# Splitting the FFN head's weights during the output projection, and adding layer 0's last squares on GpSimd

## The chip, the cores and the metric

The kernel runs on one core of a Trainium2 chip. The metric is device time in microseconds (us), from runs of the whole kernel; smaller is better. Five engines matter: TensorE (PE, with its weight load PEld), VectorE (DVE), ScalarE (ACT), GpSimd (POOL) and SyncE (SP), whose queue issues the loads. Each works through its own list of instructions in order, and semaphores tie the lists together.

## The reference, cut to what matters

Two sequences, a prompt of 256 tokens and a sample of 512, go through the same two-layer encoder in float32. Layer 0 mixes with an mLSTM, layer 1 with sliding-window attention; both end in an output projection and are followed by a convolutional feed-forward network (FFN).

```python
for l in range(DEPTH):                                   # 2 layers, d = 1024
    sh1, sc1, g1, sh2, sc2, g2 = split(silu(c) @ adaln_w[l] + adaln_b[l], 6)
    h = rmsnorm(x, norm_g[l, 0]) * (1 + sc1) + sh1
    y = mlstm_mixer(h, ...) if l == 0 else swa_mixer(h, ...)   # both end in "@ w_out"
    x = x + g1 * y
    h = rmsnorm(x, norm_g[l, 1]) * (1 + sc2) + sh2
    x = x + g2 * conv_ffn(h, w_up[l], conv_w[l], conv_b[l], w_down[l])
return rmsnorm(x, final_g)

def conv_ffn(h, w_up, conv_w, conv_b, w_down):           # 1024 -> 2 * 2816 -> 1024
    u = depthwise_conv3(h @ w_up, conv_w) + conv_b
    return (silu(u[..., :D_FF]) * u[..., D_FF:]) @ w_down

def rmsnorm(x, g):
    return x * rsqrt(mean(x * x, axis=-1) + 1e-6) * g
```

## The kernel before

The 768 tokens lie along the free dimension; channels lie on the 128 partitions, eight blocks of them (KC = 8). A float32 product is made of three matmuls: every operand is split into a high part, rounded by a cast on ACT, and a low part, the subtraction of the high part on DVE (`fp_copy_split`, L223 to L234: the cast is L232, the subtraction L233). Weights come in units of 128 x 1024 by `load` (L241) into five `raw` buffers, and `split` writes their parts into three pairs `whi`, `wlo`.

A planner orders most of the program: it lays the instructions of each engine by its own estimates of their times, so that an operation that is given to another engine also changes where its neighbours stand. In `head` the lists of PE, ACT and DVE are kept in the order in which the code is written (`manual_schedule`), while POOL and SP stay with the planner.

The places that matter here are these.

- `out_proj` (L558): the output projection of a layer, 16 tiles of 24 matmuls, eight for tokens 0 to 383, then eight for tokens 384 to 767. Each tile is followed by its residual on DVE (L557) and the square of the new x on ACT (L104); six of eight squares are summed by five adds (L108), and a mean on PE (`pa<-inv,nt`), the reciprocal root on POOL (L127, `nr`) and a broadcast on PE (`pa<-kct,nr`) make the norm's factor. The generator hands control back once, ahead of its last tile.
- `head` (L1184): the start of the FFN's first pair of up-projections. It multiplies in quarters, by a Strassen-like scheme: T1, T2, T3, T4, B22 are combinations of quarters of the activations (`zh`, `zl` hold their parts; `yh`, `yl` those of the first half), and five sums and differences of weight quarters (`sums`, L1220 to L1225) take the place of further products. `wa`, `wb`, `wc` are split weights of the pair's two units. Four products of whole weights with the first half, the outsets, start before the second half's norm is known: with wa[0], wa[1], ahead[0] and ahead[1]. While they run, the second half's norm advances step by step on DVE and ACT: T1 (four steps), four scalings, T2, T4, B22, T3 (L1054 to L1100, the low parts at L1072).
- In layer 0 the output projection reads its input from other buffers, so that `zh` and `zl` are free until the quarters are written; in layer 1 it reads `zh` and `zl` themselves.
- `ffn`, `down` (from L1362): the down-projection of the last part. Per range of 256 tokens, eight tiles of six matmuls, residual, square, add, and then the norm of the next layer (layer 0) or of the output (layer 1). The norm of layer 1 writes `zh`, `zl` with L517 (scaling on DVE), L519 (ACT) and L520 (the low part on DVE).
- After layer 0's FFN comes the attention's input projection; around its first tiles DVE and ACT also work on its keys and bias (L825 to L864).

## Time and profile before

| what | value |
|---|---|
| median of 3 runs | 1913.54 us (1912.68 to 1914.77) |
| profiled execution | 1916.43 us |
| its span, first to last instruction | 1914.6 us (1.8 us lie around it) |
| mean granted TensorE clock | 0.987 |
| PE busy | 1832.8 us (96%) |
| DVE, ACT, POOL busy | 1402.9, 909.9, 473.9 us |

The stages that the change touches lie, by the trace's timeline, at 452 to 527 us (layer 0's output projection), 523 to 564 (its FFN's head), 1030 to 1100 (the end of layer 0's FFN and the start of the attention's projection), 1302 to 1367 (layer 1's output projection) and 1363 to 1405 (its head). A row of a timeline has the start, the duration, the engine, the line, the operation with its output and inputs by the program's names, the shape, the count, and in brackets the idle time of the engine ahead of it with what ended it. A row of windows has a stretch of time, its length, the busy time of PE, PEld, DVE, ACT and POOL with the number of instructions, the granted clock, the busy share of the DMA engines and their GB/s.

### The profile page before, as it was taken

Reading aid. Unit: us, or ns where it says so; the run is one execution under the profiler, and the core shown is the slowest. Engines: PE = TensorE matmul, PEld = TensorE weight load, DVE = VectorE, ACT = ScalarE, POOL = GpSimd, SP = SyncE. Lnnn points to the kernel's source line nnn. Section 1 sums busy time; section 2 is a strip of 40 time slices with the busy share of each in tenths; the row PEclk is TensorE's granted clock in tenths of the full one; section 3 lists DMA queues with packets and bytes.
Section 4 is the critical chain, followed back from the end, with each engine's and each line's share of the span. In section 5 each row is a group of like instructions: output and inputs, shape, how many; then the busy total and the mean of one; then the engine's idle time right before and its main releaser. Section 6 shows DMA issues by size and latency. Waiting matters only on the chain.

```text
span 1914.6 us, 29030 instructions
## 1 busy us (share of the span) xinstructions
PE 1832.8 (96%) x11270; PEld 1668.4 (87%) x11270; DVE 1402.9 (73%) x2311; ACT 909.9 (48%) x1832; POOL 473.9 (25%) x372
## 2 busy tenths in 40 slices
PE   6999999999999999999999899999989999999997
PEld 4978887889988999999999798778979999999996
DVE  4765577685699777777777855775997777777777
ACT  3444333433564444444444555674565444444443
POOL 2101001021023333333331011331133333333322
PEclk9999999999999999999999899999999999999998
DMA  8343466455222212122223221122222222222112
GB/s 327 108 149 126 148 202 201 160 170 182 67 68 71 69 58 67 66 68 69 71 69 101 80 68 60 40 88 67 89 77 67 67 69 69 72 67 67 66 34 67
DMA packets 63957, 183.43 MB, mean 96 GB/s; under 512 B 6135, under 2 KB 23799, under 8 KB 63820
## 3 DMA queue, kind: packets, MB, share of 16 engines
q1 hardware_dynamic: 63820, 181.58, 28.9%
q8 instruction: 88, 1.44, 0.3%
q14 instruction: 49, 0.40, 0.1%
HBM read 175.13 MB, written 6.43 MB: 95 GB/s over the span
## 4 chain that ended last, share of the span: by engine, by line
PE 78%; DVE 10%; issue 4%; DMA 3%; ACT 3%; POOL 1%; SPq 0%; POOLq 0%; ACTq 0%; DVEq 0%
PE pa L226 25%; PE ps L226 23%; PE ps L1114 9%; PE ps L1115 9%; PE ps L1116 9%; PE pa L953 2%; DVE wlo L233 2%; DVE slab L557 1%; DMA raw<-in_adaln_w_dram 1%; DVE slab L1332 1%; ACT whi L232 1%; DVE zl L1072 1%; DMA slab<-in_x_dram 1%; DMA raw<-in_w_dram 1%; DMA slab<-in_adaln_w_dram 1%
## 5 line engine op out<-in xcount | busy, mean ns | idle before, releaser
L232 ACT CAST whi<-raw 128x1024 fp32r<-128x1024 f32 x237 | 248.4, 1049 | 419.4 <-PE pa L226 201.5
L233 DVE TENSOR_TENSOR wlo<-raw,whi 128x1024 fp32r<-128x1024 f32 x237 | 325.1, 1373 | 136.8 <-ACT whi L232 135.6
L226 PE MATMUL pa<-slab,whi 128*128 128x256 f32 (+1 forms) x1472 | 346.5, 332 | 5.7 <-DVE slab L557 5.5
L226 PEld LDWEIGHTS pa<-slab,whi 128*128 128x128 f32 x1472 | 252.2, 189 | 32.7 <-DVE slab L557 7.5
L557 DVE SCALAR_TENSOR_TENSOR slab<-pa,mod,slab 128x256 f32<-128x256 f32 (+1 forms) x368 | 207.3, 590 | 65.7 <-PE pa L226 65.4
L226 PE MATMUL ps<-zh,whi 128*128 128x256 f32 (+2 forms) x688 | 229.6, 337 | 5.3 <-ACT whi L232 4.3
L226 PE MATMUL pa<-slab,wlo 128*128 128x256 f32 (+1 forms) x736 | 234.5, 331 | 0.0
L226 PE MATMUL ps<-zh,wlo 128*128 128x256 f32 (+2 forms) x688 | 229.5, 337 | 3.8 <-DVE wlo L233 3.8
L226 PE MATMUL ps<-zl,whi 128*128 128x256 f32 (+2 forms) x688 | 230.0, 336 | 0.0
L1114 PE MATMUL ps<-zh,whi 128*128 128x384 f32 x504 | 171.6, 341 | 16.6 <-ACT ps L1169 15.5
L1115 PE MATMUL ps<-zl,whi 128*128 128x384 f32 x504 | 170.9, 339 | 1.3 <-DVE zl L1072 1.0
L1116 PE MATMUL ps<-zh,wlo 128*128 128x384 f32 x504 | 169.7, 337 | 0.0
L226 PEld LDWEIGHTS pa<-slab,wlo 128*128 128x128 f32 x736 | 139.2, 189 | 13.4 <-DVE wlo L233 0.9
L226 PEld LDWEIGHTS ps<-zh,whi 128*128 128x128 f32 x688 | 132.4, 193 | 18.6 <-ACT whi L232 6.0
L226 PEld LDWEIGHTS ps<-zh,wlo 128*128 128x128 f32 x688 | 132.9, 193 | 14.9 <-DVE wlo L233 4.6
L226 PEld LDWEIGHTS ps<-zl,whi 128*128 128x128 f32 x688 | 132.8, 194 | 10.7 <-issue 1.5
L1358 POOL TENSOR_TENSOR slab<-slab 128x772 f32<-128x772 f32 x44 | 83.6, 1901 | 205.6 <-DVE slab L1332 192.9
L1145 POOL TENSOR_TENSOR raw<-raw,raw 128x512 f32<-128x512 f32 x40 | 52.7, 1317 | 294.0 <-DVE wlo L233 244.1
L1331 DVE SCALAR_TENSOR_TENSOR slab<-slab,cstt,slab 128x771 f32<-128x771 f32 x88 | 103.5, 1178 | 26.9 <-ACT slab L1329 26.9
L1332 DVE SCALAR_TENSOR_TENSOR slab<-slab,cstt,slab 128x771 f32<-128x771 f32 x88 | 120.4, 1368 | 0.8
L476 DVE SCALAR_TENSOR_TENSOR ada<-raw,silc,ada 128x1024 f32<-128x1024 f32 x84 | 111.3, 1357 | 7.4 <-DMA raw<-in_adaln_w_dram 7.0
L1114 PEld LDWEIGHTS ps<-zh,whi 128*128 128x128 f32 x504 | 95.0, 189 | 24.5 <-ACT ps L1169 20.6
(301 smaller groups left out, 4149.6 us busy)
## 6 DMA issues: line engine op xcount, KB each, us to landing
raw<-in_w_dram SPq DMA_DIRECT2D x206, 512.0 KB, 3.7
raw<-in_adaln_w_dram SPq DMA_DIRECT2D x84, 512.0 KB, 4.4
slab<-in_x_dram SPq DMA_DIRECT2D x12, 512.0 KB, 8.3
slab<-in_adaln_w_dram SPq DMA_DIRECT2D x12, 512.0 KB, 10.2
slab<-mrows SPq DMA_DIRECT2D x8, 384.0 KB, 5.2
xs<-slab SPq DMA_DIRECT2D x6, 512.0 KB, 3.4
bt<-brow SPq DMA_DIRECT2D x16, 192.0 KB, 3.1
slab<-xs SPq DMA_DIRECT2D x6, 512.0 KB, 8.0
```

The source lines that it names most:

```text
L226: self.nc.tensor.matmul(out, lhsT, rhs, start=start, stop=stop)
L232: nc.scalar.copy(hi, src)
L233: return nc.vector.tensor_tensor(lo, src, hi.bitcast(F32), ALU.subtract)
L476: stt(acc[:, s], row, w, acc[:, s], ALU.mult, ALU.add)
L557: self.nc.vector.scalar_tensor_tensor(x, o, self.mod[l][:, gc + c, q : q + 1], x, ALU.mult, ALU.add)
L1114: mm(o, wh[:, k], hi[k], start=start and k == 0, stop=False, skip_group_check=True)
L1115: mm(o, wh[:, k], lo[k], start=False, stop=False, skip_group_check=True)
L1116: mm(o, wl[:, k], hi[k], start=False, stop=k == 3, skip_group_check=True)
L1145: tt(q[0], q[2], q[0], ALU.subtract)
L1331: stt(y[:, 1:], u[:, :-1], w(0), y[:, 1:], ALU.mult, ALU.add)
L1332: stt(y[:, :-1], u[:, 1:], w(2), y[:, :-1], ALU.mult, ALU.add)
L1358: nc.gpsimd.tensor_tensor(y, y, yrow[:, j], ALU.mult)
```

## The change

There are three edits.

1. `out_proj` hands control back once more, after its first eight tiles, and `ffn` first calls the new `prepare`, then goes on with the projection. `prepare` splits weights of the head: wa[1] (there wa2), and in layer 0 also ahead[0] and ahead[1]. In layer 0 the parts go to `zh` and `zl`, to the places that T2, T4 and T3 take later; in layer 1 wa2 goes to the `spare` slab and the two others are still split in `head`, into `zh` and `zl`. One unit per layer is loaded twice, since `sums` overwrites its raw form.
2. In `head` wc[0] is split right after the first `sums`, ahead of the projection's last tile, and wc[1] right after the second `sums`, ahead of the norm's steps. In layer 1 ahead[0] is split before the first outset.
3. The adds of squares of layer 0's last down-projection (three norms of five adds) go from VectorE to GpSimd.

```diff
@@ -577,7 +577,7 @@
 
         self.turn = 1
         for i, (z, c, w) in enumerate(tiles()):
-            if i == 2 * KC - 1:
+            if i in (KC, 2 * KC - 1):
                 yield
             c0, c1, _ = HALVES[z]
             o = self.ps()[:, : c1 - c0]
@@ -1181,34 +1181,42 @@
         self.quarters(d, part(wb, 1), self.T4, False)
         self.evict(r2, d)
 
-    def head(self, u0, last_tile, pool, urows, mark, swap):
+    def prepare(self, u0, l):
+
+        flat = [z.rearrange("p j k t -> p (j k t)") for z in (self.zh, self.zl)]
+        place = lambda j: [z[:, j : j + 1024] for z in flat]
+
+        ahead = [place(12 * H), place(4 * H)]
+        wa = place(0)
+        spare = None
+        if l:
+
+            spare = self.slab([P, 3072], R)
+            wa = [spare[:, 1024 * (z + 1) : 1024 * (z + 2)] for z in range(2)]
+        self.fp_copy_split(*wa, self.load(u0 + 1, 0))
+        for i in range(0 if l else 2):
+            self.fp_copy_split(*ahead[i], self.load(u0 + 3 + i, 0))
+        return wa, ahead, spare
+
+    def head(self, u0, last_tile, pool, urows, mark, early):
 
 
         nc = self.nc
         part = lambda w, i: [t[:, 512 * i : 512 * (i + 1)] for t in w]
-
-        spare = self.slab([P, 3072], R)
-        flat = [z.rearrange("p j k t -> p (j k t)") for z in (self.zh, self.zl)]
-        ahead = [
-            [spare[:, 1024 * (z + 1) : 1024 * (z + 2)] for z in range(2)],
-            [z[:, 12 * H : 12 * H + 1024] for z in flat],
-        ]
-
-        if swap:
-            ahead.reverse()
+        wa2, ahead, spare = early
+        done = spare is None
+        spare = spare or self.slab([P, 3072], R)
         s1 = [
             [pool.tile([P, 512], R, tag=t, name=self.nm(t), bufs=1) for t in ("s1h", "s1l")],
             [spare[:, 512 * z : 512 * (z + 1)] for z in range(2)],
         ]
         rows = [[urows[0][:, 2 * i + j] for j in range(2)] for i in range(2)]
-        ah, ra, rb = [None] * 2, [None] * 2, [None] * 2
-        ah[0] = self.load(u0 + 3, 0)
+        ra, rb = [None] * 2, [None] * 2
         ra[0], rb[0] = (self.load(u0, h) for h in range(2))
-        ra[1] = self.load(u0 + 1, 0)
-        ah[1] = self.load(u0 + 4, 0)
-        rb[1] = self.load(u0 + 1, 1)
+        ra[1], rb[1] = (self.load(u0 + 1, h) for h in range(2))
+        ah = [None if done else self.load(u0 + 3 + i, 0) for i in range(2)]
         q = [[t[:, 512 * i : 512 * (i + 1)] for t in ab for i in range(2)] for ab in zip(ra, rb)]
-        wa, wc, wb = [None] * 2, [None] * 2, [None] * 2
+        wa, wc, wb = [None, wa2], [None] * 2, [None] * 2
         fixed = lambda i: self.bank[i][:, :H]
         banks = [[fixed(i) for i in (1, 2, 3)]]
         for t in banks[0][1:]:
@@ -1233,18 +1241,19 @@
         tt = nc.vector.tensor_tensor
         p5, u3 = ([self.tmp([P, H]) for _ in range(2)] for _ in range(2))
         wa[0] = self.split(ra[0])
-        self.fp_copy_split(*ahead[0], ah[0])
         sums(0)
-        wa[1] = self.split(ra[1])
+        wc[0] = self.split(ra[0])
         for _ in last_tile:
             pass
         norm = self.take(HALVES[1])
         step = lambda n=1: [next(norm, None) for _ in range(n)]
+        if not done:
+            self.fp_copy_split(*ahead[0], ah[0])
         first = self.outset(fixed(0), wa[0], rows[0][0])
         next(first)
-        wc[0] = self.split(ra[0])
         step()
         sums(1)
+        wc[1] = self.split(ra[1])
         next(first, None)
 
         step()
@@ -1252,13 +1261,11 @@
         second = self.outset(pa(), wa[1], rows[1][0])
         next(second)
         step()
-        wc[1], low = split(ra[1])
         third = self.outset(pa(), ahead[0], urows[1][:, 0])
         next(third)
         step()
-        low()
-        _, low = split(ah[1], ahead[1])
-        low()
+        if not done:
+            self.fp_copy_split(*ahead[1], ah[1])
         next(second, None)
         step()
         next(third, None)
@@ -1316,6 +1323,8 @@
     def ffn(self, l, xt, pool, last_tile, apply, keep=None):
         nc = self.nc
         u0 = U_FFN + l * NPART * 3
+        early = self.prepare(u0, l)
+        next(last_tile)
 
         urows = [self.slab([P, 4, TG]) for _ in range(2)]
         for urow in urows:
@@ -1338,7 +1347,7 @@
                 eng = mybir.EngineType
                 self.ready(HALVES[0])
                 with self.tc.manual_schedule(engines={eng.PE, eng.Activation, eng.DVE}):
-                    behind[:] = self.head(u0, last_tile, pool, urows, mark, l == 0)
+                    behind[:] = self.head(u0, last_tile, pool, urows, mark, early)
             for i in range(2):
                 if p:
                     rows = [urow[:, 2 * i + j] for j in range(2)]
@@ -1388,7 +1397,7 @@
                 return
             ws = list(ws)
             for rng in RANGES:
-                norm = Norm(self, xt, rng, apply, last=keep is None and rng is RANGES[-1], adds=nc.vector)
+                norm = Norm(self, xt, rng, apply, last=keep is None and rng is RANGES[-1], adds=None if keep is not None else nc.vector)
                 for c in range(KC):
                     tile(ws[c // 4], c, rng)
                     norm.square(c)
```

The planner's lists show what moves. In layer 0's output projection the three casts and subtractions of `prepare` stand in the middle of the first half, among the residuals, squares and weight splits of its tiles. DVE in layer 0's head, from the first `sums`' end to the norm's first steps; before:

```order
L233 TENSOR_TENSOR wlo_5116<-raw_5091,whi_5115 128x1024
L557 SCALAR_TENSOR_TENSOR slab_4494<-ps_4486,mod_88,slab_4494 128x384
L233 TENSOR_TENSOR wlo_5160<-raw_5087,whi_5159 128x1024
...
L1225 TENSOR_TENSOR raw_5095<-raw_5095,raw_5091 128x512
L1054 TENSOR_TENSOR dsh<-mod_88 128x4
L1059 SCALAR_TENSOR_TENSOR slab_5200<-slab_4494,gain_91,pa_5196 128x384
L1076 SCALAR_TENSOR_TENSOR bq_4847<-slab_5200,mod_88,bq_4847 128x384
...
L1072 TENSOR_TENSOR zl<-bq_4854,zh 128x384
L1231 TENSOR_TENSOR wlo_5225<-raw_5091,whi_5224 128x1024
L1231 TENSOR_TENSOR slab_5082<-raw_5093,slab_5082 128x1024
L1059 SCALAR_TENSOR_TENSOR slab_5200<-slab_4494,gain_91,pa_5196 128x384
```

and with the change (lines from L1193 on are numbered up to 9 higher):

```order
L1233 TENSOR_TENSOR raw_5099<-raw_5099,raw_5097 128x512
L233 TENSOR_TENSOR wlo_5122<-raw_5097,whi_5121 128x1024
L557 SCALAR_TENSOR_TENSOR slab_4494<-ps_4486,mod_88,slab_4494 128x384
...
L1233 TENSOR_TENSOR raw_5103<-raw_5103,raw_5101 128x512
L233 TENSOR_TENSOR wlo_5185<-raw_5101,whi_5184 128x1024
L1054 TENSOR_TENSOR dsh<-mod_88 128x4
L1059 SCALAR_TENSOR_TENSOR slab_5206<-slab_4494,gain_91,pa_5202 128x384
L1076 SCALAR_TENSOR_TENSOR bq_4859<-slab_5206,mod_88,bq_4859 128x384
...
L1072 TENSOR_TENSOR zl<-bq_4866,zh 128x384
L1059 SCALAR_TENSOR_TENSOR slab_5206<-slab_4494,gain_91,pa_5202 128x384
L1076 SCALAR_TENSOR_TENSOR bq_4880<-slab_5206,mod_88,bq_4880 128x384
```

The first `wlo` there was wa[1]'s and is wc[0]'s now; the subtraction behind the last tile's residual is gone, wc[1]'s stands ahead of the first step (L1059), and none stands among the steps.

On POOL in the same head, around the reciprocal root of the second half (`nr_5173`, `nr_5175` with the change):

```order
 L809 TENSOR_TENSOR sg_4444<-sg_4444,slab_659 128x512
 L809 TENSOR_TENSOR sg_4474<-sg_4474,slab_659 128x256
-L127 TENSOR_TENSOR nr_4813<-nr_4813,mhalf 128x3
-L1322 MEMSET slab_5076 128x4x4
-L1322 MEMSET slab_5077 128x4x4
-L127 TENSOR_TENSOR nr_5173<-nr_5173,mhalf 128x3
+L127 TENSOR_TENSOR nr_4825<-nr_4825,mhalf 128x3
 L1142 TENSOR_TENSOR raw_5537<-raw_5537 128x512
+L1331 MEMSET slab_5088 128x4x4
+L1331 MEMSET slab_5089 128x4x4
 L1145 TENSOR_TENSOR raw_5539<-raw_5537,raw_5539 128x512
+L127 TENSOR_TENSOR nr_5175<-nr_5175,mhalf 128x3
```

Two of the next pair's weight sums (L1142, L1145) stand now ahead of the reciprocal root.

Last, DVE at the end of layer 0, around the third norm (`nr_9926`; L517 with `pa_9954` is its scaling). Before:

```order
L520 SCALAR_TENSOR_TENSOR zl<-nt_9815,mod_89,zh 128x256
L108 TENSOR_TENSOR nt_9736<-nt_9736,nt_9835 128x256
L520 SCALAR_TENSOR_TENSOR zl<-nt_9819,mod_89,zh 128x256
L520 SCALAR_TENSOR_TENSOR zl<-nt_9823,mod_89,zh 128x256
L126 TENSOR_SCALAR nr_9926<-pa_9919 128x2
L827 TENSOR_TENSOR slab_9873<-ps_9894,slab_9873 64x512 x2
L827 TENSOR_TENSOR slab_9874<-ps_9929,slab_9874 64x512 x2
L517 SCALAR_TENSOR_TENSOR nt_9957<-slab_4494,gain_92,pa_9954 128x256
L517 SCALAR_TENSOR_TENSOR nt_9961<-slab_4494,gain_92,pa_9954 128x256
```

and with the change:

```order
L520 SCALAR_TENSOR_TENSOR zl<-nt_9815,mod_89,zh 128x256
L520 SCALAR_TENSOR_TENSOR zl<-nt_9819,mod_89,zh 128x256
L126 TENSOR_SCALAR nr_9926<-pa_9919 128x2
L520 SCALAR_TENSOR_TENSOR zl<-nt_9823,mod_89,zh 128x256
L517 SCALAR_TENSOR_TENSOR nt_9957<-slab_4494,gain_92,pa_9954 128x256
L517 SCALAR_TENSOR_TENSOR nt_9961<-slab_4494,gain_92,pa_9954 128x256
L517 SCALAR_TENSOR_TENSOR nt_9965<-slab_4494,gain_92,pa_9954 128x256
...
L517 SCALAR_TENSOR_TENSOR nt_9985<-slab_4495,gain_92,pa_9954 128x256
L827 TENSOR_TENSOR slab_9873<-ps_9894,slab_9873 64x512 x2
L520 SCALAR_TENSOR_TENSOR zl<-nt_9957,mod_89,zh 128x256
```

The adds are gone from the list (five of them stand on POOL per norm), and the third norm's scaling stands ahead of the work on the attention's bias and keys (L827). On PE the third mean stands 40 instructions earlier, the broadcast behind it 34.

## The prediction

> **What bounds the kernel now.** I read the page first, then the windows by stage, then the timeline of TensorE (PE) at each place where it stood idle, and last the rows of the engines that ended those gaps.
>
> ```profile
> span 1914.6 us, 29030 instructions
> PE 1832.8 (96%) x11270; PEld 1668.4 (87%) x11270; DVE 1402.9 (73%) x2311; ACT 909.9 (48%) x1832; POOL 473.9 (25%) x372
> ```
>
> PE is the bound: all its idle time is 1914.6 - 1832.8 = 82 us, and the change alters no product. So it can win only idle PE time, or PE time at a lowered clock. The windows show where that is, in the stages that the change touches (stretch, length, then busy time of PE, PEld, DVE, ACT, POOL, and the granted clock):
>
> ```profile
> 452.00:523.00 71.00, 70.89 (x412) 70.73 (x413) 45.52 (x80) 32.02 (x58) 2.05 (x4) 1.00 0.40 134
> 534.00:564.00 30.00, 26.58 (x139) 23.78 (x140) 29.20 (x47) 19.80 (x42) 7.52 (x5) 1.00 0.16 53
> 1048.00:1078.00 30.00, 26.73 (x190) 25.74 (x191) 22.62 (x57) 14.49 (x33) 1.41 (x2) 0.89 0.28 94
> 1078.00:1100.00 22.00, 16.91 (x117) 15.30 (x116) 16.64 (x34) 10.62 (x21) 0.70 (x1) 0.87 0.24 77
> 1375.00:1405.00 30.00, 26.54 (x138) 23.13 (x137) 29.20 (x45) 19.30 (x41) 7.79 (x5) 1.00 0.16 53
> 1060.00:1062.00 2.00, 2.00 (x13) 2.00 (x12) 2.00 (x6) 0.86 (x3) 0.00 (x0) 0.52 0.00 0
> ```
>
> In layer 0's output projection (452 to 523) PE is full and VectorE (DVE) has 25 us free. In the two heads (534 to 564 and 1375 to 1405) it is the other way round: DVE is busy 29.2 of 30 and PE loses 3.42 and 3.46 us. At the end of layer 0 PE loses 3.27 and 5.09 us, and there the clock is lowered as well: (1 - 0.89) x 30 + (1 - 0.87) x 22 = 6.2 us of speed. The gaps themselves (last bracket: idle time before the row, and what ended it):
>
> ```profile
> 553.44 0.44 PE L1114 MATMUL ps<-bq,whi 128*128 128x384 f32 x1 [1.23 <-ACT bq L1095]
> 563.38 0.44 PE L1116 MATMUL pa<-zh,wlo 128*128 128x384 f32 x1 [1.26 <-DVE wlo L1231]
> ...
> 1048.74 0.94 PE L226 MATMUL pa<-inv,nt 128*128 128x2 f32 x7 [0.95 <-DVE nt L108]
> 1059.62 0.51 PE L226 MATMUL pa<-slab,whi 128*128 128x256 f32 x2 [1.76 <-DVE slab L557]
> 1075.84 0.39 PE L226 MATMUL ps<-zh,whi 128*128 128x256 f32 x1 [0.74 <-ACT whi L232]
> 1091.42 0.63 PE L226 MATMUL pa<-zh,whi 128*128 128x256 f32 x3 [2.29 <-ACT zh L519]
> 1092.61 1.01 PE L226 MATMUL pa<-oh,rb 33*16 33x512 f32 x2 [0.56 <-PE pa L226]
> 1094.81 0.79 PE L226 MATMUL pa<-slab,slab 128*128 128x256 f32 x2 [1.19 <-ACT bs L864]
> 1096.66 0.58 PE L226 MATMUL pa<-zl,whi 128*128 128x256 f32 x1 [1.05 <-DVE zl L520]
> ...
> 1404.27 0.45 PE L1116 MATMUL pa<-zh,wlo 128*128 128x384 f32 x1 [1.27 <-DVE wlo L1231]
> ```
>
> **The change, part by part.** First the head of layer 0, on ScalarE (ACT), DVE and GpSimd (POOL):
>
> ```profile
> 525.39 1.05 ACT L232 CAST whi<-raw 128x1024 fp32r<-128x1024 f32 x1
> 526.92 0.17 ACT L124 ACTIVATE nr<-pa 128x3 f32<-128x3 f32 x1 [0.48 <-PE pa L226]
> 528.33 0.62 ACT L1221 CAST slab<-raw 128x512 fp32r<-128x512 f32 x1 [1.24 <-DVE raw L1220]
> 526.47 1.22 DVE L233 TENSOR_TENSOR wlo<-raw,whi 128x1024 fp32r<-128x1024 f32 x1 [2.93 <-ACT whi L232]
> 529.67 0.68 DVE L1224 TENSOR_TENSOR slab<-raw,slab 128x512 fp32r<-128x512 f32 x1
> 531.07 0.61 DVE L1059 SCALAR_TENSOR_TENSOR slab<-slab,gain,pa 128x384 f32<-128x384 f32 x1
> 531.71 1.52 DVE L1076 SCALAR_TENSOR_TENSOR bq<-slab,mod,bq 128x384 f32<-128x384 f32 x1
> 533.79 0.62 DVE L1076 SCALAR_TENSOR_TENSOR bq<-slab,mod,bq 128x384 f32<-128x384 f32 x1
> 536.44 1.22 DVE L1231 TENSOR_TENSOR wlo<-raw,whi 128x1024 fp32r<-128x1024 f32 x1
> 537.68 1.22 DVE L1231 TENSOR_TENSOR slab<-raw,slab 128x1024 fp32r<-128x1024 f32 x1
> 561.01 2.31 DVE L1231 TENSOR_TENSOR wlo<-raw,whi 128x1024 fp32r<-128x1024 f32 x1
> 527.17 1.23 POOL L127 TENSOR_TENSOR nr<-nr,mhalf 128x3 f32<-128x3 f32 x1 [6.19 <-ACT nr L124]
> 531.53 1.28 POOL L1142 TENSOR_TENSOR raw<-raw 128x512 f32<-128x512 f32 x1 [3.13 <-DVE dsh L1054]
> ```
>
> From 531.07, where the norm's steps begin, DVE runs almost without a gap to the last low weight half, which ends at 563.32 and ends PE's 1.26 us wait. The change takes the two subtractions at 536.44 and 537.68 out of that run: 2 x 1.22 = 2.44 us. The run also starts earlier. Today DVE stands 2.93 us for a cast that ACT has queued behind a copy of PE's last tile; the change puts that cast ahead of it. The next bound is the cast of the sum, which follows the mean on ACT: 526.92 + 0.17 + 0.62 = 527.7. Behind it come two sums of 0.7 and the low half of wc[1] (1.2), so the steps begin at about 530.3, 0.8 earlier. Lead: 2.44 + 0.8 = 3.2 us, against 3.42 us of idle PE to be had. Some steps of the run wait for copies of PE's own results, which come no sooner; I take **-2.6** (between 1.5 and 3.3).
>
> What was removed has to be done elsewhere: three casts (1.05) and three subtractions (1.22) go into the projection's first half, 3.15 us on ACT and 3.66 us on DVE against 39 and 25 us free there, and 512 KB are loaded once more. PE is covered as long as the weights of the next tile come first. Without that cover a tile's evict would come 2 to 3 subtractions late, at most 2.4 us. I take **0** (up to +1.2).
>
> The change adds one kind of wait. T2, T4 and T3 are written where the weights of the second, third and fourth outset now lie, so DVE's low halves of these quarters (and all its steps behind them) wait for those products. In PE's order the second and third outset stand ahead of both products with T1, the end of the fourth between the two, and DVE writes T2 only after T1 and four scalings: **0**.
>
> In layer 1 only one split leaves the head (wa2), but the order changes alike: wc[1]'s subtraction moves ahead of the steps, ahead[1]'s stays.
>
> ```profile
> 1377.79 1.22 DVE L1231 TENSOR_TENSOR zl<-raw,zh 128x1024 fp32r<-128x1024 f32 x1
> ```
>
> So the run is shorter by 1.22 and starts about 0.8 earlier: 2.0 us of lead, less than the 3.46 of idle. The 1.27 us gap at 1404.27 should stay in part. I take **-1.7** (1.0 to 2.0).
>
> Then the boundary. The group of the adds on POOL exists in the trace, at the start of the kernel; beside it the same adds on DVE, then the rows that the third norm rests on:
>
> ```profile
> L108 POOL TENSOR_TENSOR nt<-nt,nt x10: 722/724/733, 7.9 to 24.6; 128x256 f32<-128x256 f32 x10
> L108 DVE TENSOR_TENSOR nt<-nt,nt x15: 409/415/427, 1044.9 to 1080.0; 128x256 f32<-128x256 f32 x15
> ...
> 1080.00 0.41 DVE L108 TENSOR_TENSOR nt<-nt,nt 128x256 f32<-128x256 f32 x1
> 1077.47 0.42 ACT L104 ACTIVATE nt<-slab 128x256 f32<-128x256 f32 x1 [0.43 <-DVE slab L557]
> 1090.86 3.30 ACT L519 ACTIVATE zh<-nt,mod 128x256 fp32r<-128x256 f32 x8
> ```
>
> An add costs 0.72 instead of 0.41 us, but stands in a queue that is otherwise empty: 15 x 0.41 = 6.2 us leave DVE. The gap at 1048.74 waits for the last add of the first norm; it is no longer behind residuals but longer by 0.31: -0.25. At 1059.62 PE waits for a residual that stands behind six norm operations and an add; one add and the reordered rows: -1.3. At 1075.84 a weight cast comes late; it stands earlier on ACT now: -0.7. The third norm counts most. Its last square ends at 1077.9, but its last add runs at 1080.00 behind the second norm's work. With the add on POOL the means stand 40 PE instructions sooner (at 0.12 us about 4.8 us), the reciprocal root follows 34 instructions sooner, and the eight casts at 1090.86 can run while PE still has products. The four waits at 1091 to 1097 sum to 5.09 us; I take 3.5 of them, since the one on the bias copy (1.19) has another cause: -3.5. Together **-5.75** (3 to 8).
>
> The clock is lowered after the gaps at 1048.74, 1059.62 and 1091 to 1097, yet stays at 1.00 after the 1.23 and 1.26 us gaps of the head, so a gap's length alone does not tell. Of 6.2 us I take a quarter, **-1.5** (0 to 4.3, the share behind the second and third place). [...]
>
> Against this stand two costs, the first with these rows of DVE's timeline and of the page's groups and DMA issues:
>
> ```profile
> 521.69 1.22 DVE L233 TENSOR_TENSOR wlo<-raw,whi 128x1024 fp32r<-128x1024 f32 x1
> L1145 POOL TENSOR_TENSOR raw<-raw,raw 128x512 f32<-128x512 f32 x40 | 52.7, 1317 | 294.0 <-DVE wlo L233 244.1
> raw<-in_w_dram SPq DMA_DIRECT2D x206, 512.0 KB, 3.7
> ```
>
> In layer 0 the reciprocal root (527.17) now stands on POOL behind two operations of the next pair, and the second (L1145) needs a load whose buffer is freed by the low half of wc[0]. That takes the place of the operation at 521.69, 1.22 sooner since a split ahead of it is gone, and ends at about 521.7; load and add bring it to 521.7 + 3.7 + 1.3 = 526.7, just in time. The load can be later: **+0.4** (0 to 5.6, where the subtraction stays at 526.47). And POOL holds DVE up: 1.52 at 531.71 beside 0.62 at 533.79, while POOL worked from 531.53. Fifteen adds of 0.72 could cost DVE up to 10.8 us at the boundary if all met such an operation, but DVE has 7.4 us free from 1048 to 1078, and most residuals wait for PE anyway: **+0.4** (0 to 3).
>
> Sum: -2.6 + 0 - 1.7 - 5.75 - 1.5 + 0.4 + 0.4 = **-10.75 us**. The profiled execution took 1916.43 us, so 1905.7 in its like; it lies 2.9 above the median of 1913.54, so the median should be 1902.8.
>
> **Rivals.** (1) *The boundary keeps its stall.* PE then waits at other rows between 1085 and 1100, for the bias copy or the low halves (zl), and only the heads and the gaps at 1059 and 1075 give: -4.3 - 2.0 + 0.8 = -5.5, 1908.0. For it: the four waits have three different ends; against it: the first and largest follows from the late add. (2) *The heads are paced by PE's copies*, so the lead turns into idle DVE: -7.0 + 0.6 = -6.4, 1907.1. DVE's 29.2 of 30 us speaks against it. (3) *The clock dips vanish too*: another -4 to -5, 1898.3. [...] (5) *It does not do what it says*, because the moved splits delay PE's projection: +2.4 there, 1905.2, within the range.
>
> **How the numbers follow.** Forecast 0.52; (1) 0.18; (2) 0.10; (3) 0.10; (4) 0.06; (5) 0.04. The time is the forecast's, 1902.8. Its own bounds are about -4.5 to -16; with the rivals 1897 to 1910 leaves out (4), the low part of (3) and the worst of (1). About 0.2% (3.8 us) is what a measurement can tell here. Faster: the forecast but for a little, (2), (3), (5), and most of (1), 0.83; within 0.2%, 0.12; slower, 0.05.
>
> **What would show it.** Right: DVE's first norm step 0.8 earlier and PE idle under 1.2 us in layer 0's head, about 1.7 in layer 1's; in the projection PE still full; the third norm's means without a wait, the wait on zh gone and under 2 us idle in the last 20 us of the boundary. Wrong: a gap ahead of `pa<-kct,nr` in layer 0's head (late reciprocal root), means that wait for `nt` from POOL with the clock at 0.5 behind them, or the 5 us stall again ahead of `pa<-zh,whi`.

## The result, and the profile after

The changed kernel takes 1898.98 us (median of 4 runs, 1896.54 to 1904.33) against 1913.11 us (4 runs, 1911.58 to 1914.77): 14.1 us less, a ratio of 0.993 with a 95% interval of 0.9907 to 0.9953. The forecast was 1902.8 us, 10.75 us less, with a range of 1897 to 1910.

The profiled execution is the longest of the four, 1904.33 us. The first lines of its page:

```profile
span 1902.5 us, 29053 instructions
PE 1830.7 (96%) x11270; PEld 1667.5 (88%) x11270; DVE 1399.1 (74%) x2296; ACT 910.3 (48%) x1832; POOL 490.3 (26%) x387
```

The span fell by 12.1 us. To see where, six rows of TensorE's timeline that stand in every kernel cut the span into stages: the projection's first matmul that waits for `sg`, the first pair's matmul that waits for ACT's copy L1169, the residual at the boundary's start (0.43), and the first product of layer 1's output projection; then the second and third again in layer 1. In the changed kernel they are:

```profile
454.52 0.62 PE L226 MATMUL ps<-slab,whi 128*128 128x384 f32 x2 [0.53 <-ACT sg L808]
575.55 0.44 PE L1114 MATMUL ps<-zh,whi 128*128 128x384 f32 x1 [1.28 <-ACT ps L1169]
1029.38 0.50 PE L226 MATMUL pa<-slab,whi 128*128 128x256 f32 x2 [0.43 <-DVE slab L557]
1289.80 0.79 PE L226 MATMUL ps<-zh,whi 128*128 128x384 f32 x3 [0.90 <-ACT zh L232]
1401.88 0.44 PE L1114 MATMUL ps<-zh,whi 128*128 128x384 f32 x1 [1.27 <-ACT ps L1169]
1854.54 0.51 PE L226 MATMUL pa<-slab,whi 128*128 128x256 f32 x2 [0.43 <-DVE slab L557]
```

and in the kernel before they start at 452.11, 575.04, 1031.23, 1302.22, 1415.93 and 1868.41. The stages (us; the experiments' columns are read in the next section):

| stage | before | after | e1 | e2 | e3 | e4 | e5 | e6 | e7 | e8 |
|---|---|---|---|---|---|---|---|---|---|---|
| up to the first row | 452.1 | 454.5 | 447.9 | 451.2 | 447.5 | 447.6 | 448.1 | 449.9 | 451.5 | 450.8 |
| layer 0: projection and head | 122.93 | 121.03 | 121.23 | 123.17 | 122.99 | 122.45 | 122.42 | 119.28 | 121.20 | 122.56 |
| layer 0: rest of the FFN | 456.2 | 453.8 | 456.7 | 456.9 | 456.3 | 456.5 | 455.3 | 452.7 | 456.1 | 452.8 |
| boundary and attention | 270.99 | 260.42 | 268.63 | 260.48 | 263.80 | 267.98 | 260.44 | 260.47 | 260.32 | 263.57 |
| layer 1: projection and head | 113.71 | 112.08 | 112.26 | 113.62 | 113.60 | 114.88 | 112.18 | 109.36 | 114.56 | 112.90 |
| layer 1: rest of the FFN | 452.5 | 452.7 | 452.4 | 452.7 | 452.6 | 450.5 | 452.7 | 451.1 | 453.2 | 452.9 |
| tail | 46.2 | 48.0 | 46.7 | 45.3 | 45.3 | 45.3 | 45.2 | 48.1 | 46.1 | 45.2 |

So the two executions differ by -1.90 in layer 0's head, -10.57 at the boundary and -1.63 in layer 1's head, together -14.1, as much as the medians do. The other stages, whose work the change leaves alone, differ by +2.4, -2.4, +0.2 and +1.8; from kernel to kernel they scatter by as much (the first by 7 us), and nothing is read into them. A part of this is the clock: from 684.7 to 688.0 us, in the rest of layer 0's FFN, it is 0.50 in the kernel before and 1.00 in the changed one. That dip is worth 0.50 x 3.3 = 1.7 us, and one like it stands in a stage of the change: e8's head in layer 0 has the changed kernel's waits, but a clock of 0.91 over its last 18 us (matmuls of 0.52 instead of 0.34 us from 560.5 to 563.7), and takes 122.56 us. So a stage is read together with its waits.

The boundary, in windows of 72 us that begin with its stage. The first row is of the kernel before, the second of the changed one:

```profile
1031.00:1103.00 72.00, 62.81 (x434) 58.64 (x435) 56.56 (x122) 31.27 (x64) 3.96 (x4) 0.91 0.26 83
```

```profile
1029.00:1101.00 72.00, 68.38 (x517) 64.93 (x518) 58.82 (x117) 37.71 (x77) 18.30 (x19) 0.98 0.31 98
```

Idle PE time falls from 9.2 to 3.6 us and the clock rises from 0.91 to 0.98, which is (0.98 - 0.91) x 72 = 5.0 us of speed. Both together are the stage's 10.6. The lowered clock lies in few places. Before the change it is 0.79 from 1047 to 1055, behind the first mean, 0.83 from 1055 to 1065, behind the second norm's residual, and 0.76 from 1089 to 1103, behind the four waits; after it, it is 0.79 from 1045 to 1053 and 1.00 from there to 1101. Its gaps now, with those of the heads:

```profile
531.87 0.93 PE L226 MATMUL pa<-kct,nr 128*128 128x128 f32 x6 [0.39 <-POOL nr L127]
563.89 0.44 PE L1116 MATMUL pa<-zh,wlo 128*128 128x384 f32 x1 [1.26 <-DVE wlo L1239]
...
1046.92 1.50 PE L226 MATMUL pa<-inv,nt 128*128 128x2 f32 x12 [0.93 <-POOL nt L108]
1056.32 0.51 PE L226 MATMUL pa<-slab,whi 128*128 128x256 f32 x2 [0.74 <-DVE slab L557]
1057.89 0.39 PE L226 MATMUL ps<-zl,whi 128*128 128x256 f32 x1 [0.24 <-DVE zl L520]
1060.45 0.61 PE L226 MATMUL pa<-inv,nt 128*128 128x2 f32 x4 [0.76 <-POOL nt L108]
...
1366.91 0.44 PE L1116 MATMUL pa<-yh,zl 128*128 128x384 f32 x1 [0.64 <-DVE zl L233]
1380.28 0.44 PE L1114 MATMUL ps<-bq,whi 128*128 128x384 f32 x1 [0.51 <-ACT bq L1095]
1390.22 0.45 PE L1116 MATMUL pa<-zh,wlo 128*128 128x384 f32 x1 [1.25 <-DVE wlo L1239]
```

One more wait for a low half, of 0.17 us, stands at 1058.68. The four waits at 1091 to 1097 (5.09 us) are gone, all of them. The wait for the first norm's last add has only changed its engine (0.95 on DVE, 0.93 on POOL). Layer 0's head shows the new wait for the reciprocal root (0.39) and the old one for the last low half (1.26); what went there is the wait of 1.23 us for `bq` (L1095). In layer 1 that wait is still 0.51 us, and there is a new one of 0.64 us for the low half of ahead[1].

Layer 0's head, in detail (DVE, then POOL, then one row of ACT, and last a row of DVE in the kernel before):

```profile
530.04 1.05 DVE L1232 TENSOR_TENSOR slab<-raw,slab 128x512 fp32r<-128x512 f32 x1 [1.79 <-ACT slab L1229]
532.88 1.25 DVE L1054 TENSOR_TENSOR dsh<-mod 128x4 f32<-128x4 f32 x1
534.05 0.60 DVE L1059 SCALAR_TENSOR_TENSOR slab<-slab,gain,pa 128x384 f32<-128x384 f32 x1
543.12 1.14 DVE L1085 SCALAR_TENSOR_TENSOR bq<-slab,mod,bq 128x384 f32<-128x384 f32 x2
544.58 0.56 DVE L1072 TENSOR_TENSOR zl<-bq,zh 128x384 fp32r<-128x384 f32 x1 [0.33 <-ACT zh L1066]
546.29 0.56 DVE L1072 TENSOR_TENSOR zl<-bq,zh 128x384 fp32r<-128x384 f32 x1 [0.62 <-ACT zh L1066]
548.47 0.56 DVE L1072 TENSOR_TENSOR zl<-bq,zh 128x384 fp32r<-128x384 f32 x1 [1.09 <-ACT zh L1066]
561.52 2.31 DVE L1239 TENSOR_TENSOR wlo<-raw,whi 128x1024 fp32r<-128x1024 f32 x1
...
529.25 1.30 POOL L1145 TENSOR_TENSOR raw<-raw,raw 128x512 f32<-128x512 f32 x1 [5.86 <-DMA raw<-in_w_dram]
530.51 1.31 POOL L127 TENSOR_TENSOR nr<-nr,mhalf 128x3 f32<-128x3 f32 x1
531.79 2.31 POOL L1146 TENSOR_TENSOR raw<-raw 128x512 f32<-128x512 f32 x1
561.19 1.55 POOL L1145 TENSOR_TENSOR raw<-raw,raw 128x512 f32<-128x512 f32 x1 [23.10 <-ACT zh L1066]
...
547.48 0.54 ACT L1122 COPY slab<-pa 128x128 f32<-128x128 f32 x2 [1.23 <-PE pa L1116]
...
543.04 3.01 DVE L1085 SCALAR_TENSOR_TENSOR bq<-slab,mod,bq 128x384 f32<-128x384 f32 x2
```

Counted from the stage's first row, the norm's steps (L1059) begin at 534.05 - 454.52 = 79.53 us. Before the change it was 531.07 - 452.11 = 78.96. They were to begin 0.8 sooner and begin 0.57 later: L1232 takes 1.05 us where it took 0.68, and the tiny L1054 takes 1.25 where it took 0.15, both while POOL works. On the way DVE wins some of it back where POOL is now idle: two L1085 take 1.14 us, and took 3.01 beside POOL's L1146 and L1142 before (542.77 to 545.63). Then DVE waits 0.33, 0.62 and 1.09 us for casts that stand on ACT behind copies of PE's own results; the row of ACT shows such a copy waiting for PE. And the last low half still takes 2.31 us beside POOL's L1145.

### The profile page after: what moved, and what is told of

Same layout as the page of the kernel before. It is cut to its first block, busy times and chain, and to the rows that moved or that the text cites. A ratio compares the mean times of both kernels' runs of the same rounds, so it can differ in the third digit from the quotient of the medians.

```text
span 1902.5 us, 29053 instructions
## 1 busy us (share of the span) xinstructions
PE 1830.7 (96%) x11270; PEld 1667.5 (88%) x11270; DVE 1399.1 (74%) x2296; ACT 910.3 (48%) x1832; POOL 490.3 (26%) x387
## 3 DMA queue, kind: packets, MB, share of 16 engines
q8 instruction: 88, 1.44, 0.3%
## 5 line engine op out<-in xcount | busy, mean ns | idle before, releaser
L1145 POOL TENSOR_TENSOR raw<-raw,raw 128x512 f32<-128x512 f32 x40 | 52.3, 1308 | 293.9 <-DVE wlo L233 244.3
```

The lines of the kernel that those rows point to most:

```text
L1145: tt(q[0], q[2], q[0], ALU.subtract)
```

## The experiments

Theory A: the boundary's gain hangs on the adds' engine, above all on the third norm's. Its rivals: it came through the heads' shift (B), or through VectorE time as such (A2). Theory E: in the heads, GpSimd's sums hold VectorE up. Its rival C: what paces the heads is ACT's copies of PE's results. Each experiment is compared with the kernel before in runs made beside it, so the time of the kernel before differs from one to the next.

### The boundary

e1: the changed kernel with the adds back on VectorE.

```diff
-adds=None if keep is not None else nc.vector
+adds=nc.vector
```

> The changed kernel with its third edit undone: layer 0's fifteen adds of squares are back on VectorE, the early splits and the new order in the heads stay. Theory A (the heads give what their rows show, 1.9 and 1.6 us, and the boundary's 10.6 us hang on the adds alone): 1913.1 - 3.5 = 1909.6 us, the four waits ahead of pa<-zh,whi to pa<-zl,whi there again with about 5 us and the clock near 0.5 behind them. [...]

Measured: 1910.99 us against 1914.43, 3.4 us less (ratio 0.9985, 0.997 to 0.9999), so theory A. The four waits, and the clock behind them, in its timeline and windows:

```profile
1084.45 0.62 PE L226 MATMUL pa<-zh,whi 128*128 128x256 f32 x3 [2.29 <-ACT zh L519]
1085.64 1.57 PE L226 MATMUL pa<-oh,rb 33*16 33x512 f32 x2 [0.56 <-PE pa L226]
1087.87 0.80 PE L226 MATMUL pa<-slab,slab 128*128 128x256 f32 x2 [0.67 <-ACT bs L864]
1089.69 0.58 PE L226 MATMUL pa<-zl,whi 128*128 128x256 f32 x1 [1.02 <-DVE zl L520]
...
1084.00:1098.00 14.00, 11.29 (x65) 9.35 (x66) 10.64 (x22) 6.63 (x14) 0.00 (x0) 0.76 0.15 46
```

They sum to 4.54 us. The stage is 268.63 us, 2.4 less than before, though no edit of e1 touches it: its planner's list differs a little (the wait at 1059 is 1.39 us here, the one at 1075 is 0.16), and one dip of the clock is missing.

e2: the kernel before with the third edit alone.

```diff
-adds=nc.vector
+adds=None if keep is not None else nc.vector
```

> The kernel before with the third edit alone (adds of layer 0's last squares on GpSimd). Theory A: 1913.1 - 10.6 = 1902.5 us; idle PE time from 1030 to 1100 falls from 9.4 to about 3.7 us, and the clock dips at 1060 and 1094 are gone. Rival B: under 3 us of gain, 1910 us or more. If the two parts add up, this gain and that of the kernel with the heads' part alone sum to the whole 14.1 us.

Measured: 1904.18 us, 10.25 less (0.9938, 0.9913 to 0.9962). The boundary's stage is 260.48, the changed kernel's 260.42. With e1's 3.4 the parts make 13.7 of the 14.1 us: they add up within the intervals.

e3 and e4 put the adds of one part of the norms on GpSimd, in the kernel before.

```diff
-adds=nc.vector
+adds=None if keep is not None and rng is RANGES[-1] else nc.vector
```

> The kernel before with only the third norm's five adds on GpSimd. Theory A1 (the third norm's last add, late behind the second norm's work, makes the four waits): the 5.1 us of waits at 1091 to 1097 and the lowered clock behind them (about 2.5 us) go, the gaps at 1048 and 1059 stay: 1913.1 - 7.5 = 1905.5 us. Rival A2 (what counts is the VectorE time that all fifteen adds free): a third of the gain, about 1909.5 us, with most of the four waits still there.

Measured: 1905.48 us, 8.95 less (0.9956, 0.9942 to 0.997), which is A1's number; the stage is 263.80, 7.2 less. Of the four waits one is left, and it is longer (1.86 us, 1.05 before):

```profile
1085.28 0.39 PE L226 MATMUL pa<-zl,whi 128*128 128x256 f32 x1 [1.86 <-DVE zl L520]
1085.00:1099.00 14.00, 13.72 (x102) 13.72 (x103) 12.01 (x23) 8.70 (x16) 0.00 (x0) 0.88 0.29 86
```

So 3.2 of the 5.1 us of waits went, and half of the dip behind them (0.88 instead of 0.76 over 14 us). The number fits better than its terms: behind the first mean and the second norm's residual, whose waits the edit leaves at 0.95 and 1.76 us, the clock is 1.00 in this execution, which A1 did not foresee and the edit doesn't explain.

For e4 the condition is `rng is not RANGES[-1]`.

> The kernel before with only the first and second norms' ten adds on GpSimd, the third's on VectorE. Theory A1: the gap at 1059 shrinks from 1.76 to below 0.8 us and its clock dip goes (1.0 + 1.7 us together), the four waits at 1091 to 1097 stay: 1913.1 - 2.7 = 1910.4 us. Rival A2 (freed VectorE time): two thirds of the gain, about 1906 us, with the four waits much shorter.

Measured: 1911.37 us, 3.06 less (0.9984, 0.9972 to 0.9997); the stage is 267.98, 3.0 less. The four waits are there (2.43, 0.67, 0.67, 0.76) and the clock over them is 0.76 again. The residual's wait is 0.73, as A1 said. But its dip has not gone (0.83 from 1056 to 1066), while the one behind the first mean has, though that wait is 0.98. So A1 for the waits: the third norm's five adds carry the larger part of the gain, 8.95 us against 3.06 for the ten others by the medians. The stages of single executions can't split it finer, since a dip more or less moves them by 1.7 us.

e8 asks whether the two waits that are left for adds can go too.

```diff
-adds=None if keep is not None else nc.vector)
+adds=None if keep is not None else nc.vector, on_pe=2 if keep is None else 3)
```

> The changed kernel with three squares instead of two given to the means' matmuls in layer 0's last norms, so four adds on GpSimd instead of five per norm. Theory G (the waits of 0.93 and 0.76 us ahead of the means are for the last add): both fall to about 0.3, the six matmuls more cost about 0.25 us each on one norm's path, and the boundary (270.99 us before, 260.42 with the change, from the wait of 0.43 us at its start to attention's output projection) takes 259.5; if the clock dip behind the first mean goes too, 257.8. Rival H: the means then wait for the squares themselves, and the boundary stays at 260.4 or grows by the added matmuls to 261.

Measured: 1902.4 us against 1912.21 (0.9952, 0.9936 to 0.9968), and the stage is 263.57, 3.1 longer than with the change. Neither theory had this:

```profile
1042.83 1.95 PE L226 MATMUL pa<-inv,nt 128*128 128x2 f32 x16 [0.18 <-POOL nt L108]
1084.62 0.39 PE L226 MATMUL pa<-zl,whi 128*128 128x256 f32 x1 [2.17 <-DVE zl L520]
1084.00:1098.00 14.00, 13.38 (x99) 13.38 (x100) 11.74 (x24) 8.64 (x17) 0.00 (x0) 0.88 0.39 101
```

The wait for the first norm's last add falls from 0.93 to 0.18 and the second norm's (0.76) is gone, as G said. But the dip behind the first mean stays (0.79 over 8 us), the planner lays its lists anew, and PE meets a low half 2.17 us too soon, as in e3, with the clock at 0.88 behind it.

### The heads

e5: in the changed kernel only GpSimd's list is altered, so that the reciprocal root stands ahead of the next pair's sums as it did before.

```diff
-nc.gpsimd.tensor_tensor(r, r, net.mhalf[:, :nb], ALU.pow)
+net.pow = nc.gpsimd.tensor_tensor(r, r, net.mhalf[:, :nb], ALU.pow)
...
-for ins in behind[2 * i :] if p == 1 else ():
+for ins in [*behind[2 * i :], self.pow.ins] if p == 1 else ():
```

> The changed kernel with GpSimd's list alone put back in one place: the reciprocal root of the second half's norm stands again ahead of the next pair's weight sums (L1142, L1145), in both layers. The stage is measured in the trace from the projection's first matmul that waits for ACT's sg to the pair's first matmul that waits for ACT's copy L1169: 122.9 us before, 121.0 with the change in layer 0. Theory C (VectorE's steps run ahead until they meet casts that stand behind ACT's copies of PE's own results, so a late start is absorbed): only the 0.39 us wait for the root goes, 120.6 us. Rival D (the 1.4 us by which the steps start late carry through to the head's end): 119.2 us.

Measured (one run, 1898.2 us against 1912.21): layer 0's stage is 122.42 us, 1.4 longer than with the change, so neither. The root is in time, and PE stands still elsewhere (DVE, then PE):

```profile
524.35 1.65 DVE L1233 TENSOR_TENSOR raw<-raw,raw 128x512 f32<-128x512 f32 x1
525.92 2.31 DVE L233 TENSOR_TENSOR wlo<-raw,whi 128x1024 fp32r<-128x1024 f32 x1
528.16 1.25 DVE L1054 TENSOR_TENSOR dsh<-mod 128x4 f32<-128x4 f32 x1
529.33 0.60 DVE L1059 SCALAR_TENSOR_TENSOR slab<-slab,gain,pa 128x384 f32<-128x384 f32 x1
...
531.56 0.45 PE L1114 MATMUL pa<-yh,zh 128*128 128x384 f32 x1 [1.67 <-ACT slab L1129]
```

All three sums of POOL now run against DVE's last operations ahead of the steps; these take 1.65, 2.31 and 1.25 us where DVE without POOL takes 0.69, 1.22 and 0.15. The steps begin at 529.33 - 448.11 = 81.22, ACT's first cast of T1 waits for them, the copy behind it (L1129) too, and PE for that copy's buffer.

e6: the changed kernel without the second pair's weight sums on GpSimd; that pair multiplies unsummed weights.

```diff
-tt = nc.gpsimd.tensor_tensor
+tt = (lambda *z: None) if rest else nc.gpsimd.tensor_tensor
```

> The changed kernel without the weight sums of the FFN's second pair on GpSimd (five sums and differences per unit, both layers; that pair then multiplies unsummed weights, so part of the output is not the reference's). GpSimd is idle in both heads but for the reciprocal root. Theory E (the last low half, L1239, is slow at 2.31 us because GpSimd reads at the same time): it takes 1.22 us, the wait of 1.26 us ahead of the matmul that needs it falls to about 0.2, and with the root in time the stage is 121.0 - 1.5 = 119.5 us in layer 0 and 112.1 - 1.1 = 111.0 in layer 1. Rival C (the steps ahead of it are paced by ACT's copies alone): the wait stays over 1 us, 120.6 and 112.1.

Measured (one run, 1892.77 us against 1912.21): the stages are 119.28 and 109.36 us. Three rows of layer 0:

```profile
527.99 0.61 DVE L1059 SCALAR_TENSOR_TENSOR slab<-slab,gain,pa 128x384 f32<-128x384 f32 x1
556.28 1.22 DVE L1239 TENSOR_TENSOR wlo<-raw,whi 128x1024 fp32r<-128x1024 f32 x1
557.55 0.44 PE L1116 MATMUL pa<-zh,wlo 128*128 128x384 f32 x1 [0.17 <-DVE wlo L1239]
```

The last low half takes 1.22 us and PE waits 0.17: theory E. The steps begin at 527.99 - 449.90 = 78.09, which is 0.87 sooner than before the change; the forecast had said 0.8. But C has its part: DVE then waits 1.32, 0.62 and 1.09 us for the same casts, which is 0.99 more than with the change, so most of the 1.44 us by which its steps begin sooner is idle time.

e7: the changed kernel with the second edit undone.

```diff
 sums(0)
-wc[0] = self.split(ra[0])
 ...
 next(first)
+wc[0] = self.split(ra[0])
 ...
-wc[1] = self.split(ra[1])
 ...
+wc[1], low = split(ra[1])
 third = self.outset(pa(), ahead[0], urows[1][:, 0])
 ...
+low()
```

> The changed kernel with its second edit undone: wc[0] is split again after the first outset's first half and wc[1] among the norm's steps; the early splits during the projection and the adds on GpSimd stay. Theory F (what counts is how much VectorE work leaves the run of steps): 1.2 us instead of 2.4 are gone in layer 0 and none in layer 1, so the stages take 122.9 - 1.2 = 121.7 and 113.5 us. Rival (the early splits alone bring the gain, the order nothing): 121.0 and 112.1.

Measured (one run, 1904.89 us against 1912.21): 121.20 and 114.56 us. In layer 0 the early splits bring the whole gain without the order, as the rival said; in layer 1 there is none, as F said, and a wait of 0.88 us for a low half more. Layer 0 does not tell that the order is worth nothing: in e7 POOL's list is another, with the root ahead of L1145. Its two L1085 take 2.02 us instead of 3.01, since one of POOL's sums runs beside them and not two, and the lead that the order would give meets the same casts.

e9 and e10 try to keep e6's gain with nothing left out. A one-column memset on VectorE, then one on GpSimd, holds the second pair's sums back: in e9 the first unit's until T1 is done and the second unit's until the low half of wb[1], in e10 the second unit's alone.

```diff
+def gate(i):
+    z = self.dsh[:, 4 + i : 5 + i]
+    nc.vector.memset(z, 0.0)
+    self.gates[i] = [nc.gpsimd.memset(z, 1.0).ins]
...
 fork(0)
+gate(0)
...
 low()
+gate(1)
...
-for ins in behind[2 * i :] if p == 1 else ():
+for ins in [*behind[2 * i :], *self.gates[i]] if p == 1 else ():
```

> The changed kernel with the second pair's weight sums on GpSimd moved, nothing left out: the first unit's (L1142, L1145, L1146) start only when VectorE has done step T1 (a one-column memset on each engine makes the order), the second unit's only when the low half of wb[1] is done. Theory E (in the heads GpSimd's reads hold VectorE up): the norm's steps begin 78.1 us after the stage's start as without GpSimd's sums, not 79.5; what the first unit costs then falls into the 3 us that VectorE waits for casts anyway; the last low half takes 1.22 instead of 2.31 us. Stages 119.4 and 109.6 us against 121.0 and 112.1 with the change: 4 us faster than it, about 1895 us. Rival I (the sums come too late for the pair that needs them): the wait of 1.3 us ahead of the pair's first matmul grows by 1 to 2 us and the stages stay at 120.5 to 121.5 and 112.

> The changed kernel with only the second unit's weight sums held back until the low half of wb[1] is done; the first unit's stay ahead of the reciprocal root. Theory E: the last low half takes 1.22 us and the wait of 1.26 us behind it falls to 0.2, while the late start remains: stages 119.9 and 111.0 us, about 2.2 us faster than the changed kernel, 1896.8 us. Rival C (the last steps are paced by ACT's copies): 121.0 and 112.1, no gain.

Measured: 1901.05 us for e9 (0.9924, 0.9908 to 0.9941) and 1901.84 for e10 (0.9932, 0.9915 to 0.9949), both against 1914.73: no better than the change's 0.993. The rows of e9 show both halves of the story (DVE, then PE):

```profile
523.25 0.61 DVE L1060 SCALAR_TENSOR_TENSOR slab<-slab,gain,pa 128x384 f32<-128x384 f32 x1
551.54 1.22 DVE L1240 TENSOR_TENSOR wlo<-raw,whi 128x1024 fp32r<-128x1024 f32 x1
556.97 4.02 DVE L1350 SCALAR_TENSOR_TENSOR slab<-slab,cstt,slab 128x771 f32<-128x771 f32 x2
...
552.82 0.44 PE L1117 MATMUL pa<-zh,wlo 128*128 128x384 f32 x1 [0.16 <-DVE dsh L1246]
565.07 0.45 PE L1115 MATMUL ps<-zh,whi 128*128 128x384 f32 x1 [1.88 <-ACT ps L1170]
574.16 0.44 PE L1115 MATMUL ps<-zh,s1h 128*128 128x384 f32 x1 [1.99 <-DVE slab L1181]
```

(The gate's lines shift the line numbers here by one: L1060 is L1059, L1170 is L1169.) The steps begin at 523.25 - 445.20 = 78.05 and the last low half takes 1.22 us, as theory E said. But POOL's sums now meet DVE in the pair behind: two operations of the convolution take 4.02 us (2.98 with the change), and PE waits 1.88 and 1.99 us there where it waited 1.28 and 0.91. The stage is 119.87 us in layer 0 and 111.53 in layer 1 for e9, 120.59 and 111.14 for e10. Measured on to the residual of the first down-projection (616.35 with the change), layer 0 takes 161.83 us with the change, 162.77 in e9 and 163.00 in e10, so all of it is given back. A part of that is a dip of the clock, worth 1.7 us, behind one of these waits (0.50 from 574.9 to 578.2 in e9 and from 570.4 to 573.7 in e10, where the changed kernel's pair has 1.00). But the waits alone are enough: in layer 1 e9 has them too (1.92 and 1.98 us) at a clock of 1.00, and from the stage's first row to the same residual (1442.65 with the change) it takes 154.00 us, 152.85 with the change. Rival I.

No variant that does the whole work was shown to be faster than the changed kernel. What stays open: why the clock is lowered behind some waits of about a microsecond and not behind others, and which order would save the low half in e8.

## Why the prediction was right

The time lies within the range, 3.8 us below the forecast, and its direction and its largest places were right. It lies nearer to the third rival (1898.3, the dips vanish too), which had a chance of 0.10. Its signs came true at the boundary's end, where the third norm's means have no wait, the wait on `zh` is gone and PE has no gap from 1063 to 1101 us. They did not in the heads: PE's idle time in 30 us fell to 1.9 and 3.0 us only, and DVE's steps began later and not sooner. And two things came that had been named signs of being wrong: PE's gap ahead of `pa<-kct,nr` (0.39 us), and a first mean that waits for POOL's `nt` with the clock lowered behind it. By its own steps:

- **Layer 0's head, -2.6 and +0.4 for the root: measured -1.90.** The sum held better than its working, and in part by luck. The root was late by the 0.39 us that had been allowed. The step that failed is "the steps begin at about 530.3": it took durations from a stretch in which POOL was idle for one in which, by the order, POOL would work. The cost that POOL puts on DVE had been counted at the boundary alone. GpSimd's sums turned the 0.8 us of earlier start into 0.57 us of delay; e6 shows the earlier start as it had been reckoned, 0.87 us. What made up for it was not in the working either: the two L1085 that POOL no longer meets, 1.9 us. DVE then lost 2.04 us waiting for casts behind ACT's copies, which was the second rival's mechanism. So the lead of 3.2 us did not come about. PE's wait for the last low half, which it was to shorten, stayed at 1.26, and what PE gained is the 1.23 us wait for `bq` (L1095) and some smaller ones, less the late root.
- **The splits in the projection, 0.** From 454.52 to 531.87 PE has no gap over 0.2 us, so the cover was there.
- **Layer 1's head, -1.7: measured -1.63.** The wait for the last low half stayed, as said (1.25 us). Its cause is not the steps' pace but POOL: in e6 it falls with POOL's sums, and the stage by 2.7 us more. The new wait of 0.64 us for ahead[1]'s low half is not in the working.
- **The boundary's idle time, -5.75: measured -5.7** by the gaps (9.36 us of listed waits before, 3.66 after), with other parts: the four waits gave 5.09 instead of 3.5, and new waits of 0.24, 0.17 and 0.76, with 0.5 us less from the first two gaps, took the difference. The bias copy's wait (1.19) was no wait of another cause; it went with the rest, and in e1 and e4, where the third norm is late, it is back at 0.67. That the third norm's late add is the root was right: in e3 three of the four waits go with its five adds alone.
- **The clock, -1.5: measured -5.0** (0.91 to 0.98 over 72 us). This is the term that was mis-sized, and its 3.5 us are nearly the whole distance to the result. Only a quarter of the 6.2 us was taken because a gap's length did not tell a dip. Of the 5.0, (1 - 0.76) x 14 = 3.4 us lay behind the four waits. The clock was 0.76 there in each of the three kernels that have them (before, e1, e4), so this share could have been taken whole. The other (1 - 0.83) x 10 = 1.7 us lay behind the residual's wait, and that they went is not shown to be the change's doing: the clock there is 1.00 in e1 and e3 too, with waits of 1.39 and 1.76 us. Together that is 5.1 us, three dips of 1.7.
- **POOL against DVE at the boundary, +0.4, and the fourth rival (slower, 0.06).** POOL's adds were held up, DVE was not delayed so that PE would show it: three adds of the changed kernel take 1.91, 1.53 and 1.92 us instead of 0.72, beside low halves, while a residual that runs beside an add keeps its 0.48 and the add its 0.74.

```profile
1058.49 1.91 POOL L108 TENSOR_TENSOR nt<-nt,nt 128x256 f32<-128x256 f32 x1 [3.57 <-ACT nt L104]
1052.17 0.74 POOL L108 TENSOR_TENSOR nt<-nt,nt 128x256 f32<-128x256 f32 x1 [0.61 <-ACT nt L104]
1052.22 0.48 DVE L557 SCALAR_TENSOR_TENSOR slab<-pa,mod,slab 128x256 f32<-128x256 f32 x1 [0.71 <-PE pa L226]
```

The low half takes 1.22 us alone (e6) and 2.31 beside POOL's L1145; the residual, which reads PE's result `pa`, does not grow: 0.48 us beside an add, and 0.48 at 1049.75, where POOL is idle.

## What to carry to other kernels

Where an engine's queue holds one short operation that a later stage needs, behind work for another stage, look for an empty queue even if the operation is slower there: 0.72 instead of 0.41 us per add took 10 us off, most of it through five adds. Price a step with the durations of the engines that will run beside it in the new order, not of those beside it now; between VectorE and GpSimd that was up to 1.1 us for each operation in the heads here, whether it takes 0.15 or 1.22 us alone. Where the same waits have the same dip of the clock in every trace, count it whole. And a lead that an engine wins is worth no more than the next thing that it waits for, so follow the lead to the end of the stage and beyond: e9 gained 1.2 us in the head and lost them in the pair behind.

## What the runs showed of the hardware

A VectorE operation of 0.15 us on four columns (L1054; 0.15 in the kernel before, e6 and e7) took 1.25 us beside GpSimd in the changed kernel and in e5, and the low half on 128x1024 took 2.31 instead of 1.22 us in both heads of the kernel before and of the changed one: an overlap costs 1.1 us in both cases, so it is no share of VectorE's own time. It was 0.1 to 0.2 us less than what was left of the GpSimd operation that had started ahead: in the changed kernel L1145 ends at 561.19 + 1.55 = 562.74, 1.22 us after the low half has begun (561.52), and the low half takes 1.09 us longer. For L1054 it is 1.10 of 1.22 us, for L1232 of the changed kernel 0.37 of 0.51, for L1076 of the one before 0.90 of 1.10. GpSimd's operations there take 1.3 to 1.65 us; L1146 takes 2.31 us at 531.79 and 2.16 at 562.83, where VectorE's low half had started ahead of it, and 1.29 at 542.77 in the kernel before.

At these places the granted clock is 0.50 or 1.00 and nothing between: 0.50 from 1050.0 to 1053.0, from 1060.2 to 1063.4 and from 1094.3 to 1101.0 in the kernel before. A mean of 0.79 over 8, 0.83 over 10 or 0.88 over 14 us is one such dip, worth 1.7 us, and 0.76 over 14 us is two. The dips behind single waits are not decided by their length: the wait of 1.76 us ahead of the second norm's residual has 0.83 behind it over 10 us in the kernel before and 1.00 in e3, and the first mean's wait of about 0.95 has 0.79 over 8 us in the kernel before, the changed one, e1, e2 and e7, and 1.00 in e3 and e4. In e5, e9 and e10 the matmuls on 128x256 behind it take 0.41 us for about 3 us, and in e6 0.28. In e8, where the wait is only 0.18, the 0.79 stands all the same. What decides it no run here shows, nor whether it makes the scatter of 7 us in a stage that no edit touches.
